# A gathered expert stage: side work emitted more thinly, one head routed alone, a fifth of the output sums on VectorE

## The chip, the cores and the metric

The kernel runs on one core of a Trainium2 chip. The metric is the device time of one execution in microseconds (us). A core has five instruction queues that matter here: PE (TensorE, matrix products), DVE (VectorE), ACT (ScalarE), POOL (GpSimd, which also issues the gathers) and SP (SyncE, which issues the weight loads). Each executes its instructions in the order fixed when the kernel is built. 16 DMA engines, shared by all queues, move data from memory.

## The reference, cut to what matters

Two transformer blocks run on 256 tokens of width 1024. The first ends in a PEER layer, a lookup in 16384 experts:

- For each token and each of 8 heads, a query is scored against two sets of 128 subkeys. The 16 best of each set give 256 candidate sums, of which the 16 best name 16 experts, with a softmax over their scores as gates ("routing").
- For each of the 8 x 16 = 128 experts of a token, the row `u` (1024 numbers) is multiplied with the token's vector and summed, passed through gelu and multiplied with the gate. The row `v` of that expert, times this number, is added to the token's output.

The second block starts with an mLSTM mixer. It treats a context of 256 tokens, which does not depend on the first block, and then the 256 tokens of the first block's output, which start from the context's final state. A mixture of 16 experts, a retention mixer and a second mixture of experts follow.

## The kernel before, in words

Tokens lie in two tiles of 128, one token per partition. The PEER stage (`peer`, L1227) has three pieces of work.

- `prepare` (L1241): eight steps, one per head. A step multiplies the tokens with a 1 MB slab of query weights on PE (L1247), copies the result, multiplies it with the subkeys, and ACT copies the scores to `sc` (L1258). Each weight half is first split into two parts by ACT and by a subtraction on DVE or POOL (L599, tile `rw`). After steps 1, 3 and 7, `route` is called for tile 0 with heads 0 to 1, 2 to 3 and 4 to 7 (L1268). After the last step tile 1 is routed, four heads at a time (L1270). Routing is almost wholly DVE work: L1343 is its first instruction and the cast at L1423 its last, which writes the row numbers for the gathers.
- `picks` (L1274): for each tile, 128 picks in pairs. POOL issues an indirect DMA (L1294) that fetches 8 KB (`u` and `v`) for each of the 128 tokens, 1 MB in all, into one of six ring buffers. DVE multiplies the `u` half with the tokens and sums (L1295, recorded at L608 as a 128x1024 instruction). Once per pair, ACT applies gelu and DVE the gate. For each pick, ACT then scales an identity matrix by the 128 weights and PE multiplies it with the `v` half, in two halves of 512 columns, summed over the 128 picks in two PSUM banks (L1305). After a tile's last pick the sum is added to `self.x[i]` (L1308).
- `context_task` (L1517): the mixer's context part. It loads the context (`load_context`, L1458), normalises it, multiplies it with 17 slabs of 1 MB (query, key, value, gates, output), and does the attention-like part for eight heads.

These three are written down in one order by `drive` (L795): every pick is worth 2600 units, and for each unit times `PACE` the side work (`prepare`, then `context_task`) is advanced by as many units as its steps claim (5200 for a slab, for example). With `PACE` 0.45 that is 1170 units per pick. Where a pick needs a head that is not routed yet, `prepare` is advanced until it is. `weave` interleaves two pieces of work in the same way.

The order written down is not the final one. When the program is built, a scheduler orders each engine's instructions: it keeps every dependency through data and through reused memory, and among what it takes to be ready it goes by the order written down. Work written late can therefore stand early on its engine, once the memory that it uses is free. Memory is handed out in the order written: `load_context` comes after the routing of tile 1 there, and its buffers reuse that routing's (offsets 8192 and up of `fa`).

The program lists each engine's work by helper lines: L592 is any ACT operation, L599 a tensor_tensor, L608 a scalar_tensor_tensor, L611 a matmul and L621 a transpose.

Of the kernel before, what the change touches and what calls it, by code (L numbers as in the profile page):

```python
# [15 lines left out]
OP = mybir.AluOpType  # L16
# [5 lines left out]

RING, BATCH = 6, 2

PACE = 0.45

RESERVE = (600, 1800)

# [465 lines left out]
class K:  # L494
# [732 lines left out]
    def peer(self):  # L1227
        h2, g = self.f(2048, True), self.bcast_row("ffn")
        self.ada_steps(99)
        self.mc = self.f(128, True)  # L1230
        h2T = self.norm_T([x.a for x in self.x], self.col("g_ffn"), sums=self.sq.a[:, :8], rows=(g, h2))
        self.sq.free(), g.free()
        self.mod_cols(0, [(n, b) for n in range(2) for b in range(2)])
        self.mod_cols(1, [(0, 0), (1, 0)])
        self.routes = [{"heads": 0, "rows": self.f(128), "gate": self.f(128), "act": self.f(128)} for _ in range(2)]
        prep = self.prepare(h2T)
        main = self.picks(h2, prep)
        self.drive(main, [self.chain(prep, self.context_task())], PACE)
        self.stream.grow(1)

    def prepare(self, h2T):  # L1241

        self.sc = [self.plain(self.RA) for _ in range(2)]
        sub = self.stream.get(("w1", 50))
        for s in range(8):
            w = self.wslab(("w1", 42 + s))
            p = self.slab_T(h2T, w)  # L1247
            q = self.f(512)
            self.act(q.a, p.a)
            p.free()  # L1250
            self.wfree(w)
            p = self.ps()
            for i in range(2):
                for f in range(2):
                    self.mm(p.a[:, i * 256 + f * 128:i * 256 + f * 128 + 128], q.a[:, f * 256 + i * 128:f * 256 + i * 128 + 128],
                            sub.a[:, (2 * s + f) * 128:(2 * s + f + 1) * 128])
            for i in range(2):
                self.act(self.sc[i].a[:, s * 256:(s + 1) * 256], p.a[:, i * 256:(i + 1) * 256])  # L1258
            p.free(), q.free()
            yield 5200  # L1260
            if s == 7:
                for b in h2T:
                    b.free()
                sub.free()
                self.stream.shrink(2)
                self.units.lo = deque([None])
            if s in (1, 3, 7):
                yield from self.route(0, {1: 0, 3: 2, 7: 4}[s], s + 1)  # L1268
        for h in (0, 4):
            yield from self.route(1, h, h + 4)  # L1270
        for b in self.sc:
            self.stream.give_back(b)

    def picks(self, h2, prep):  # L1274


        ident = self.c("ident")
        ring = dg = None
        for i, r in enumerate(self.routes):
            while r["heads"] < 1:  # L1280
                yield next(prep) * 0
            if ring is None:
                ring, dg = deque(self.f(2048, True) for _ in range(RING)), deque(self.f(128, True) for _ in range(2 * BATCH))
            po = self.ps(2)
            rows, gate, act = (r[n].a for n in ("rows", "gate", "act"))
            for k in range(0, 128, BATCH):
                while r["heads"] * 16 < k + 1:
                    yield next(prep) * 0
                got = []
                for j in range(k, k + BATCH):  # L1290
                    b = ring[0].a
                    ring.rotate(-1)
                    got.append(b)
                    self.nc.gpsimd.indirect_dma_start(b, None, self.t["puv"], bass.IndirectOffsetOnAxis(ap=rows.bitcast(U32)[:, j:j + 1], axis=0))  # L1294
                    self.stt(b[:, :1024], b[:, :1024], 1.0, h2.a[:, i * 1024:(i + 1) * 1024], OP.mult, OP.mult, accum_out=act[:, j:j + 1])  # L1295
                    yield 2600
                o = act[:, k:k + BATCH]
                self.act(o, o, AF.Gelu)
                self.tt(o, o, gate[:, k:k + BATCH], OP.mult)
                for j, b in enumerate(got):  # L1300
                    d = dg[0].a
                    dg.rotate(-1)
                    self.act(d, ident, AF.Copy, scale=act[:, k + j:k + j + 1])
                    for f in range(2):
                        self.mm(po.a[:, f * 512:(f + 1) * 512], d, b[:, 1024 + f * 512:1024 + (f + 1) * 512], k + j == 0, k + j == 127)  # L1305
            for f in range(2):
                o = self.x[i].a[:, f * 512:(f + 1) * 512]
                self.tt(o, po.a[:, f * 512:(f + 1) * 512], o, OP.add)  # L1308
            po.free()
            for n in ("rows", "gate", "act"):  # L1310
                r[n].free()
        h2.free()
        for b in (*ring, *dg):
            b.free()
# [1085 lines left out]
```

## Time and profile before

| | |
|---|---|
| time, median of 3 runs | 2660.72 us (2659.89 to 2661.95) |
| the profiled execution's own time | 2664.42 us |
| span of the profiled execution | 2662.7 us |
| PE busy / DVE busy / ACT busy / POOL busy | 87% / 46% / 28% / 24% |
| mean granted PE clock | 0.958 |
| bytes moved by DMA | 853.28 MB, mean 320 GB/s |
| of these by the POOL queue (the gathers, mostly) | 281.90 MB |

The shares are means over stages with different limits. The gathers lie between 421 and 1232 us of the span. Before them stands the first block (projections and weight products), after them the mixer's second part, the first mixture of experts, the retention mixer and the second mixture of experts. A row of the profile's windows gives, for a stretch of time, how long each engine was busy and with how many instructions, the granted PE clock (1.00 is 2.4 GHz, 0.50 is 1.2 GHz), the share of time in which the 16 DMA engines were busy, and the rate at which they moved bytes.

### The profile page before, as it was taken

How to read it: one execution, taken by the hardware profiler on the slowest of the kernel's cores; microseconds unless marked ns; L12 is line 12 of the kernel's file. 1: busy time of each engine (PE TensorE's matmuls, PEld its weight loads, DVE VectorE, ACT ScalarE, POOL GpSimd, SP SyncE). 2: the span in 40 equal slices, each digit the busy share in tenths (PEclk: the TensorE clock that was granted, in tenths of full speed). 3: DMA queues.
4: the chain of work that ended last, by engine and by line, in shares of the span. 5: the costliest groups of instructions: out<-in, count | busy, mean ns of one | idle time of the engine just before them, and what ended most of it. 6: DMA issues, size and time to landing. Idle time of an engine off the chain costs nothing. (4 is left out here: it accounts for less than half of the span.)

```text
span 2662.7 us, 32333 instructions
## 1 busy us (share of the span) xinstructions
PE 2304.7 (87%) x12327; PEld 1394.2 (52%) x12327; DVE 1236.1 (46%) x2823; ACT 751.5 (28%) x1492; POOL 626.5 (24%) x517
## 2 busy tenths in 40 slices
PE   8999987779978897777888999999879979878876
PEld 7888976325624573225876344443469963222213
DVE  4465358897855775556774112112286441000101
ACT  6554443224612642113543000000233520000000
POOL 4233433344344424433420000000033310000000
PEclk9999998889989999999998999999999989999999
DMA  7676557899999899995447999999966389999998
GB/s 281 215 250 227 208 189 279 327 349 351 352 381 396 311 351 378 416 419 208 152 146 280 390 391 409 409 409 409 361 223 211 120 317 384 409 409 409 409 409 276
DMA packets 195323, 853.28 MB, mean 320 GB/s; under 512 B 14558, under 2 KB 39726, under 8 KB 148832
## 3 DMA queue, kind: packets, MB, share of 16 engines
q1 hardware_dynamic: 153376, 569.31, 56.2%
q0 software_dynamic: 41792, 281.90, 27.7%
q8 instruction: 97, 1.59, 0.2%
q14 instruction: 58, 0.48, 0.0%
HBM read 849.97 MB, written 1.18 MB: 320 GB/s over the span
## 5 line engine op out<-in xcount | busy, mean ns | idle before, releaser
L611 PE MATMUL pp<-fa 128*128 128x512 f32 (+8 forms) x4900 | 1295.2, 497 | 221.4 <-ACT fa L592 156.7
L611 PEld LDWEIGHTS pp<-fa 128*128 128x128 f32 (+2 forms) x4900 | 561.1, 161 | 840.2 <-issue 439.4
L608 DVE SCALAR_TENSOR_TENSOR fa<-fa 128x1024 f32<-128x1024 f32 (+5 forms) x560 | 406.2, 748 | 170.9 <-DMA fa<-in_puv,fa 165.4
L611 PE MATMUL pp<-rw,rt 128*128 128x256 f32 x2928 | 401.2, 294 | 19.0 <-DVE fa L608 7.7
L611 PEld LDWEIGHTS pp<-rw,rt 128*128 128x128 f32 x2928 | 371.2, 196 | 44.3 <-issue 13.7
L1294 POOL DMA_INDIRECT fa<-in_puv,fa x256 | 278.6, 1088 | 432.3 <-PE pp L611 316.5
L599 DVE TENSOR_TENSOR fa<-pp,fa 128x512 f32<-128x512 f32 (+3 forms) x217 | 121.2, 565 | 510.7 <-PE pp L611 491.9
L592 ACT ACTIVATE fa<-fa 128x2 f32<-128x2 f32 (+9 forms) x476 | 188.0, 421 | 568.5 <-DVE fa L608 423.0
L611 PE MATMUL pp<-rt,rw 128*128 128x256 f32 x2448 | 329.4, 294 | 19.8 <-ACT rw L592 5.9
L611 PEld LDWEIGHTS pp<-rt,rw 128*128 128x128 f32 x2448 | 311.4, 198 | 35.8 <-issue 8.9
L592 ACT ACTIVATE fa<-pp 128x512 f32<-128x512 f32 (+4 forms) x164 | 93.9, 578 | 763.4 <-PE pp L611 600.7
L599 POOL TENSOR_TENSOR rw<-fa,rw 128x1024 fp32r<-128x1024 f32 x81 | 207.4, 2562 | 354.9 <-ACT rw L592 315.3
L592 ACT ACTIVATE rw<-fa 128x1024 fp32r<-128x1024 f32 x208 | 216.1, 1052 | 214.8 <-PE pp L611 124.3
L599 DVE TENSOR_TENSOR rw<-fa,rw 128x1024 fp32r<-128x1024 f32 x127 | 176.6, 1392 | 180.2 <-ACT rw L592 177.0
L611 PE MATMUL pp<-rt,fa 128*64 128x512 f32 (+3 forms) x736 | 239.7, 574 | 16.1 <-DMA rt<-in_moe_up 9.1
L611 PE MATMUL pp<-rw,fa 128*64 128x512 f32 (+2 forms) x720 | 206.4, 582 | 15.6 <-DMA rw<-in_moe_down 7.0
L605 DVE TENSOR_SCALAR fa<-pp,fa 128x128 f32<-128x128 f32 (+1 forms) x80 | 36.4, 462 | 256.9 <-PE pp L611 180.0
L599 DVE TENSOR_TENSOR fa<-fa 128x2 f32<-128x2 f32 (+13 forms) x311 | 100.3, 334 | 66.3 <-ACT fa L592 39.6
L611 PEld LDWEIGHTS pp<-rt,fa 128*64 128x64 f32 (+1 forms) x736 | 65.2, 124 | 116.9 <-issue 78.3
L611 PEld LDWEIGHTS pp<-rw,fa 128*64 128x64 f32 (+1 forms) x720 | 58.5, 123 | 126.0 <-issue 84.6
L621 PE MATMUL pp<-ct,fa 128*128 128x128 f32 (+3 forms) x425 | 72.6, 301 | 53.2 <-ACT fa L592 22.4
L1204 POOL DMA_DIRECT2D fa<-in_ada_b x4 | 2.3, 578 | 456.0 <-PE pp L611 456.0
(136 smaller groups left out, 1016.6 us busy)
## 6 DMA issues: line engine op xcount, KB each, us to landing
fa<-in_w SPq DMA_DIRECT2D x105, 1024.0 KB, 5.2
fa<-in_moe_gate SPq DMA_DIRECT2D x72, 1024.0 KB, 16.5
fa<-in_moe_down SPq DMA_DIRECT2D x68, 1024.0 KB, 16.1
fa<-in_moe_up SPq DMA_DIRECT2D x60, 1024.0 KB, 18.1
fa<-in_ada_w SPq DMA_DIRECT2D x48, 1024.0 KB, 5.4
rw<-in_moe_up SPq DMA_DIRECT2D x36, 1024.0 KB, 17.8
rt<-in_moe_down SPq DMA_DIRECT2D x31, 1024.0 KB, 14.9
rt<-in_moe_up SPq DMA_DIRECT2D x28, 1024.0 KB, 17.3
```

The lines of the kernel that those rows point to most:

```text
L592: return self.nc.scalar.activation(out, in_, func, **kw)
L599: (eng or self.nc.vector).tensor_tensor(out, a, b, op=op)
L605: (eng or self.nc.vector).tensor_scalar(out, a, s1, s2, op0=op0, op1=op1, **kw)
L608: self.nc.vector.scalar_tensor_tensor(out, a, s, b, op0=op0, op1=op1, **kw)
L611: self.nc.tensor.matmul(ps, l, r, start=start, stop=stop, skip_group_check=True)
L621: self.nc.tensor.transpose(ps, x, self.c("ident")[:k, :k])
L1204: self.nc.gpsimd.dma_start(b.a, self.t["ada_b"][1, :, s * 256:(s + 1) * 256])
L1294: self.nc.gpsimd.indirect_dma_start(b, None, self.t["puv"], bass.IndirectOffsetOnAxis(ap=rows.bitcast(U32)[:, j:j + 1], axis=0))
```

## The change

- `PACE` goes from 0.45 to 0.21, so a pick advances the side work by 546 units. The units of `prepare` are multiplied by 0.3, so its steps come at 1820 units per pick.
- The routing of tile 1 leaves `prepare` for a generator of its own, `prepare_last`. It is woven into `context_task`, 1.5 of its units for each of the context's. The context's work, its loads and its memory are therefore written down ahead of tile 1's routing and between its steps.
- `route` is called after steps 0, 1, 3 and 7 for heads 0, 1, 2 to 3 and 4 to 7 of tile 0.
- For every fifth pick (`SHARE` 5: picks 4, 9, ..., 124 of each tile, 25 per tile), one DVE instruction multiplies the `v` half with the weight and adds it to `self.x[i]`. The scaled identity on ACT and the matrix products on PE of that pick fall away.

```diff
-PACE = 0.45
+PACE = 0.21
+
+SHARE = 5
...
-        prep = self.prepare(h2T)
-        main = self.picks(h2, prep)
-        self.drive(main, [self.chain(prep, self.context_task())], PACE)
+        side = self.chain((0.3 * c for c in self.prepare(h2T)), self.weave(self.context_task(), [self.prepare_last()], 1.5))
+        self.drive(self.picks(h2, side), [side], PACE)
         self.stream.grow(1)
...
-            if s in (1, 3, 7):
-                yield from self.route(0, {1: 0, 3: 2, 7: 4}[s], s + 1)
+            if s in (0, 1, 3, 7):
+                yield from self.route(0, {0: 0, 1: 1, 3: 2, 7: 4}[s], s + 1)
+
+    def prepare_last(self):
+
         for h in (0, 4):
             yield from self.route(1, h, h + 4)
         for b in self.sc:
             self.stream.give_back(b)
...
                 for j, b in enumerate(got):
+                    if (k + j) % SHARE == SHARE - 1:
+                        self.stt(self.x[i].a, b[:, 1024:], act[:, k + j:k + j + 1], self.x[i].a, OP.mult, OP.add)
+                        continue
                     d = dg[0].a
                     dg.rotate(-1)
                     self.act(d, ident, AF.Copy, scale=act[:, k + j:k + j + 1])
```

## Rows read from the trace of the kernel before

**Rows 1.** All instructions by windows, 421 to 1200 us (busy us and count per engine).

```profile
core 0: us, PE busy (x) PEld busy (x) DVE busy (x) ACT busy (x) POOL busy (x), PEclk, DMA share, GB/s
421.00:500.00 79.00, 62.66 (x264) 41.56 (x264) 61.77 (x243) 27.87 (x58) 29.99 (x27) 0.87 0.88 337
500.00:600.00 100.00, 72.46 (x132) 28.69 (x133) 96.79 (x364) 20.79 (x57) 38.95 (x34) 0.85 0.90 339
600.00:750.00 150.00, 137.06 (x629) 89.51 (x627) 114.36 (x229) 75.20 (x139) 67.17 (x60) 0.94 0.94 350
750.00:850.00 100.00, 74.45 (x186) 32.20 (x187) 50.97 (x97) 17.96 (x58) 37.12 (x37) 0.97 1.00 408
850.00:1000.00 150.00, 138.68 (x674) 93.72 (x673) 114.50 (x282) 78.06 (x185) 58.32 (x57) 0.95 0.90 330
1000.00:1100.00 100.00, 75.89 (x176) 31.34 (x175) 52.04 (x109) 19.20 (x62) 44.12 (x38) 0.95 0.98 389
1100.00:1200.00 100.00, 74.05 (x162) 28.78 (x161) 52.59 (x100) 17.92 (x60) 38.02 (x41) 1.00 1.01 420
```

**Rows 2.** Gathers alone (L1294) by windows (busy us and count).

```profile
421.00:600.00 179.00, 62.46 (x56) 0.86 0.89 338
...
600.00:750.00 150.00, 50.11 (x42) 0.94 0.94 350
...
850.00:1000.00 150.00, 41.53 (x38) 0.95 0.90 330
...
1100.00:1200.00 100.00, 38.02 (x41) 1.00 1.01 420
```

**Rows 3.** Gathers (L1294), durations and extent; then who waited for whom, 421 to 1240.

```profile
L1294 POOL DMA_INDIRECT fa<-in_puv,fa x256: 935/939/3062, 421.5 to 1217.3; - x128
...
POOL fa L1294 <- PE pp L611: 316.5, 162, 10.6
DVE fa L608 <- DMA fa<-in_puv,fa: 165.4, 136, 6.2
```

**Rows 4.** Timelines of ACT, DVE, POOL and PE (start, us): routing and context start.

```profile
394.16 0.66 ACT L592 ACTIVATE rt<-pp 128x256 f32<-128x256 f32 x2 [0.49 <-PE pp L611]
398.34 0.49 DVE L1343 MAX8 fa<-rt 128x8 f32<-128x128 f32 x2 [1.40 <-PE pp L611]
399.08 0.64 ACT L592 ACTIVATE rt<-pp 128x256 f32<-128x256 f32 x2
421.07 0.18 DVE L1423 CAST fa<-fa 128x32 uint32<-128x32 f32 x1
520.38 0.19 DVE L1423 CAST fa<-fa 128x64 uint32<-128x64 f32 x1
595.20 0.20 DVE L1423 CAST fa<-fa 128x64 uint32<-128x64 f32 x1
596.45 0.59 POOL L1461 DMA_DIRECT2D fa<-in_ctx  x1
619.05 1.91 PE L621 MATMUL pp<-ct,fa 128*128 128x128 f32 x16
```

**Rows 5.** Instruction groups by form, 421 to 1240 us (count, busy us, mean ns).

```profile
L611 PE MATMUL pp<-fa 128*128 128x512 f32 x1024 | 503.5, 639 | 139.6 <-ACT fa L592 139.6
L608 DVE SCALAR_TENSOR_TENSOR fa<-fa 128x1024 f32<-128x1024 f32 x256 | 313.7, 1228 | 165.6 <-DMA fa<-in_puv,fa 165.4
L592 ACT ACT_TABLE_LOAD x40 | 51.3, 1283 | 5.0 <-DVE fa L608 4.1 <-DMA fa<-arow 0.2
L608 DVE DVE_READ_ACCUMULATOR fa<-fa 128x1 f32 x256 | 21.1, 82 | 0.0
```

**Rows 6.** PE's timeline: pairs of picks (8 matmuls each) after idle stretches.

```profile
521.45 6.18 PE L611 MATMUL pp<-fa 128*128 128x512 f32 x8 [4.33 <-ACT fa L592]
770.77 3.70 PE L611 MATMUL pp<-fa 128*128 128x512 f32 x8 [3.03 <-ACT fa L592]
1092.65 3.70 PE L611 MATMUL pp<-fa 128*128 128x512 f32 x8 [1.27 <-ACT fa L592]
```

## The prediction

> **What bounds the kernel now.** I read the page's slices first. The POOL queue's DMA share and the rate show a long stretch in which the gathers run. Then I read the windows over that stretch. In the last window, 1100 to 1200 us, the DMA engines are busy all the time and move 420 GB/s [rows 1], and 41 gathers are issued [rows 2], 2.44 us each. This is the floor. There the two longest waits of the stage are the ones that a full DMA leaves: POOL waits for a ring buffer that PE frees, DVE for a gather to land [rows 3]. Earlier windows fall below 420 GB/s although gathers are always open. The bytes that were not moved, as time at 420 GB/s (length x (1 - rate/420)):
>
> - 421 to 500: 79 x (1 - 337/420) = 15.6 us
> - 500 to 600: 19.3 us, with DVE busy 97%
> - 600 to 750: 25.0 us, with PE busy 91%
> - 750 to 850: 2.9 us
> - 850 to 1000: 32.1 us, with PE busy 92%
> - 1000 to 1100: 7.4 us
>
> The sum is 102.3 us [rows 1]. What fills these windows is the side work: routing on DVE until 595.2, the context's part on PE only after that. Its load is issued at 596.4, at the end of the routing of tile 1, whose memory it reuses, and its first PE work is at 619.05 [rows 4]. The stage's end sets the start of the mixer's second part, which needs all of `x`. What follows it doesn't touch the change, so I take every microsecond of this stage as one of the whole.
>
> **The change part by part.** The sum is made against the profiled execution: 2664.42 us, of which 2662.7 is the span and 1.7 lies around it. The median of the runs shown is 3.7 us below it.
>
> *One head routed alone.* The scores of step 0 leave ACT at 394.8, those of step 1 at 399.7 (start of the pair plus 0.64 to 0.66). Routing two heads runs from 398.34 to 421.25 on DVE, 22.9 us, with three weight residues (L599) between [rows 4]. One head has half the lists and half the elements. I take 13 us for it, a little over half, because the residues stay. Starting at about 395.5 it ends at 408.5, so the first gather comes 13 us earlier. Bounds: 17 us if the residues fall behind the routing, and nothing if the steps behind it are held back by as much. The second head's own routing then costs DVE again some 13 us, before pick 16.
>
> *Context ahead of tile 1's routing.* Today the two follow each other: routing of tile 1 from 520.38 to 595.20 on DVE, then the context's weight products on PE [rows 4]. In the change the context's memory is handed out first, so PE can start it at the end of the routing of tile 0, some 75 us earlier, beside tile 1's routing. The unmoved bytes of 500 to 600 (19.3 us) then overlap those of 600 to 750 (25.0 us). They would vanish if DVE had room for both. It has 36 us free in 600 to 750 [rows 1]. The two routings of tile 1 need about what is left of DVE's 96.8 us in 500 to 600 beside the picks (56 in 421 to 600 [rows 2], so some 31 here), for four fifths of that time: (96.8 - 31 x 1.31) x 0.8 = 45 us, with 1.31 for the 1.228 us of a dot and its read of the sum, 0.082 [rows 5]. So not all of it fits. I take 12 of 19.3; bounds 0 and 19.3.
>
> *Thinner emission.* Units worked out from the steps in the code: 129,900 for `prepare` after the first routing and 92,400 for the context, so today the side is written down until pick 190 (222,300/1170). In the change it is 24,500 (0.3 x 81,750 after head 0) plus 92,400, at 546 per pick, until pick 214; tile 1's routing is through at pick 115, before pick 128 needs it. That is thinner by 1.1 times in length, and by more in the context. But emission ranks work and does not place it: tile 1's routing, written from pick 62 to 111, was finished at 595, when not quite 56 gathers had been issued [rows 2]. So most of the side work will again stand as early as its memory allows. I take 8 us of the remaining 102 - 12 - 20 = 70; bounds 0 and 70. The moved steps bring their 17 loads of 1 MB on SP and their POOL work (context load, broadcasts, masks) with them. These stay inside the gather stage, in the same POOL queue between gathers, and cost what they do today.
>
> *Every fifth output on DVE.* It removes 50 x 4 matmuls and 50 identity scalings. At the full clock 8 matmuls of a pair take 3.70 us [rows 6], so a pick is 1.85. In 600 to 750 and 850 to 1000 PE is over 90% busy and 80 gathers are issued [rows 2]: 16 of them leave PE, 30 us. I take 20 us, because DVE is 76% busy there too; bounds 0 and 30. It adds 50 DVE instructions of 128x1024 with two inputs. The trace has none that adds into `x`; the nearest row is the dot of the same kind and size, 1.228 us, so 61 us in all; bounds 45 and 75. In the free stretches a pair asks DVE for 2 x 1.31 + 1.23 = 3.9 of its 4.88 us, so this is hidden. In 500 to 600 DVE has 3 us free, and 11 of the first 56 picks bring 14 us plus the split routing's fixed part, less the routing that moves to later windows. I put 7 us; bounds 0 and 30. The new instruction stands behind the gate product on DVE. Behind it waits the next dot, and for that PE, a pair later; six ring buffers cover 1.2 us.
>
> *Tables.* ACT loads a table 40 times (1.28 us each) where gelu and the context's exponentials alternate [rows 5]. Thinner mixing can add some, each of them in a pair's chain. At 257 us busy of 779, I put nothing; bound 20 us.
>
> Sum: -13 - 12 - 8 - 20 + 7 = -46 us. 2664.4 - 46 = 2618.4, and less the 3.7 us between that execution and the median: 2615 us. A measurement of this kernel tells a change apart from about 0.2%, 5 us.
>
> **The rivals.**
>
> *The filler really thins out* (chance 0.20). Then the side work fills only what PE and DVE have free beside gathers at the floor, and three quarters of the 102 us come back besides the 13: 90 us, 2571. For it: PE's whole work in 421 to 1200 is 635 us [rows 1], 85 of it goes, and DVE's 543 grows by some 70; both are below the time that the bytes need. Against it: the early place of tile 1's routing today.
>
> *The order hardly changes* (0.22). The side work stands as dense as before, the gathers stay behind it, and DVE takes as much as PE gives: only the earlier start and little more remain, 5 to 20 us, 2650. For it: the engines' orders follow memory and readiness more than emission. Against it: the memory that held the context back is no longer taken by tile 1's routing.
>
> *PE's clock falls* (0.13), the slower side. PE idles 1.27 us before a full pair in the free stretch, and 8 matmuls take 3.70 us. After 3.03 us of idling they took 3.70 as well, after 4.33 us they took 6.18, and the window 500 to 600, whose pairs stand far apart, has a granted clock of 0.85 [rows 1, 6]. A pair with one pick on DVE leaves 1.27 + 1.85 = 3.1 us idle, and two of five pairs are such. At the low level 8 matmuls take between the 6.18 seen and twice 3.70, say 6.8 us; ten picks with 8 on PE take 27.2 us instead of the 24.4 of the gathers, so the 150 or so free picks cost 42 us and the 20 us of relief do not come: -13 - 12 - 8 + 7 + 42 = +16, 2677. It decides once more than 26/0.28 = 93 picks run at the low level. Against it: 3.03 us did not lower it, and a PE that becomes the bound has no idle time.
> The Trainium skill (TensorE: Matmul & The Clock Gate, "HAM oscillation — how this bites in real kernels") warns of just this: where the compute between two DMA waits is shorter than the wait, the array goes back to the low clock at each. The trace agrees for 521 and not for 770 [rows 6]; by the rule the time would be the 2677 above.
>
> **How the numbers follow.** Forecast 0.45 (its own range 2600 to 2635), thinning 0.20, little change of order 0.22, the clock 0.13. The range from 2572 to 2668 takes in the third case, half of the second and a part of the last, and leaves out about 0.18. Faster by over 0.2% (below 2655): 0.45 + 0.20 + 0.13 of the third case = 0.78. Same: 0.08. Slower: the clock and a rest, 0.14.
>
> **What would show it.** The first gather near 408 instead of 421.5. The load of the context near 520 instead of 596, and its first PE work well before 619. In windows of the gather stage a rate above 360 GB/s wherever side work stands, and the last gather near 1172. 824 instead of 1024 matmuls of 512 columns in the stage [rows 5], and 50 more 128x1024 instructions on DVE of about 1.23 us. The forecast is wrong if the stretch from the first gather to the last stays near 796 us, if DVE is above 95% busy beyond 600, or if the granted clock in a free stretch falls below 0.9. After the last gather nothing should move but by the shift.

## The result, and the profile after

The change makes the kernel slower: 2697.35 us median (2690.44 to 2707.69), against 2660.82 before. The ratio is 1.0139 with an interval of [1.0121, 1.0158]. The profiled execution took 2700.99 us, its span is 2699.2. The forecast was 2615.

The page of the kernel after, parts 1 and 2: busy time per engine, and the span in 40 slices of 67.5 us.

```profile
PE 2282.6 (85%) x12127; PEld 1377.5 (51%) x12127; DVE 1293.6 (48%) x2899; ACT 744.0 (28%) x1447; POOL 659.5 (24%) x517
...
PEclk9999997888779997788899999999979989999998
DMA  7676548877899988998348799999966389999998
GB/s 282 210 254 234 200 181 324 331 296 284 310 366 416 343 337 329 379 380 319 115 134 306 302 397 409 409 409 409 387 239 237 103 343 356 409 409 409 409 409 268
```

The gather stage is slices 7 to 19. The granted clock stands at 7 or 8 tenths in ten of these thirteen slices, the late ones included, in which little side work stands.

The gathers of the kernel after: their durations (shortest, median, longest, ns), first and last start.

```profile
L1298 POOL DMA_INDIRECT fa<-in_puv,fa x256: 932/968/3829, 412.8 to 1261.3; - x128
```

The first gather comes 8.7 us earlier than in [rows 3], the last one 44.0 us later. The stage between them takes 848.5 us instead of 795.8. From the last gather to the end of the span it is 1437.9 us, before 1445.4. So the loss arises in the gather stage.

All instructions of the kernel after by windows, with the columns of [rows 1].

```profile
421.00:500.00 79.00, 60.01 (x259) 37.70 (x257) 66.86 (x216) 26.20 (x56) 30.01 (x22) 0.83 0.84 320
500.00:600.00 100.00, 77.94 (x271) 44.37 (x272) 90.65 (x307) 35.27 (x73) 45.61 (x37) 0.81 0.85 328
600.00:750.00 150.00, 112.38 (x463) 69.81 (x462) 127.46 (x324) 65.31 (x110) 58.36 (x50) 0.85 0.82 297
750.00:850.00 100.00, 66.92 (x117) 25.74 (x118) 57.29 (x101) 14.77 (x49) 42.84 (x37) 0.83 0.97 384
850.00:1000.00 150.00, 130.20 (x606) 87.90 (x606) 123.71 (x296) 69.72 (x168) 61.29 (x59) 0.92 0.93 351
1000.00:1100.00 100.00, 68.38 (x160) 28.74 (x158) 53.05 (x105) 22.09 (x58) 43.07 (x35) 0.83 0.90 348
1100.00:1200.00 100.00, 65.29 (x111) 25.44 (x112) 56.85 (x98) 13.71 (x47) 43.90 (x35) 0.79 0.95 378
1200.00:1240.00 40.00, 29.29 (x52) 11.16 (x51) 22.04 (x39) 6.25 (x21) 16.47 (x16) 0.81 0.95 369
```

Read the clock, then the rate. Between 1100 and 1200 PE, DVE and ACT are all far from full. Yet the rate is 378 GB/s where it was 420, at a clock of 0.79 where it was 1.00. The time of the bytes not moved at 420 GB/s, worked out as in the prediction, for before, after and four of the kernels below:

| window | before | after | sums alone | without the sums | thin alone | sums and zero column |
|---|---|---|---|---|---|---|
| 421–500 | 15.6 | 18.8 | 15.2 | 18.1 | 14.5 | 18.8 |
| 500–600 | 19.3 | 21.9 | 23.8 | 20.7 | 21.7 | 19.5 |
| 600–750 | 25.0 | 43.9 | 27.5 | 30.0 | 29.3 | 36.8 |
| 750–850 | 2.9 | 8.6 | 9.3 | 3.1 | 2.4 | 2.9 |
| 850–1000 | 32.1 | 24.6 | 31.4 | 33.2 | 24.6 | 22.1 |
| 1000–1100 | 7.4 | 17.1 | 8.8 | 6.4 | 3.1 | 2.6 |
| 1100–1200 | 0 | 10.0 | 12.4 | 0 | 1.0 | 2.6 |
| sum | 102.3 | 144.9 | 128.4 | 111.5 | 96.6 | 105.3 |

After the change 18.9 us more are lost in 600 to 750, and 25.4 us in the three windows that were nearly free (750 to 850, 1000 to 1200).

PE's timeline of the kernel after, two places in late windows (start, busy us, idle before in brackets). A pick on PE is 4 matmuls, 1.85 us at the full clock.

```profile
839.87 1.98 PE L613 MATMUL pp<-fa 128*128 128x512 f32 x4 [1.26 <-ACT fa L594]
844.82 3.70 PE L613 MATMUL pp<-fa 128*128 128x512 f32 x8 [2.96 <-ACT fa L594]
849.79 1.98 PE L613 MATMUL pp<-fa 128*128 128x512 f32 x4 [1.27 <-ACT fa L594]
854.76 3.70 PE L613 MATMUL pp<-fa 128*128 128x512 f32 x8 [2.99 <-ACT fa L594]
...
1125.22 11.31 PE L613 MATMUL pp<-fa 128*128 128x512 f32 x20 [4.15 <-ACT fa L594]
1142.99 11.14 PE L613 MATMUL pp<-fa 128*128 128x512 f32 x20 [6.45 <-ACT fa L594]
1157.37 3.68 PE L613 MATMUL pp<-fa 128*128 128x512 f32 x4 [3.25 <-ACT fa L594]
```

POOL's timeline over the second place.

```profile
1129.28 1.14 POOL L1298 DMA_INDIRECT fa<-in_puv,fa  x1 [6.68 <-PE pp L613]
1130.72 1.73 POOL L1298 DMA_INDIRECT fa<-in_puv,fa  x1 [0.30 <-issue]
...
1137.44 0.93 POOL L1298 DMA_INDIRECT fa<-in_puv,fa  x1 [0.30 <-issue]
```

At 840 to 860 the pattern is as hoped: a pair every 4.96 us, the full clock after gaps of 1.3 and 3.0 us. At 1157 one pick alone takes 3.68 us, twice its 1.85: the low level. Around it the pairs no longer come one by one. Twenty matmuls stand in one block of 11 us. DVE's timeline shows what held PE before the first of these blocks (dots are 128x1024, gate products 128x2; the rows that read a dot's sum are left out).

```profile
1114.96 0.16 DVE L601 TENSOR_TENSOR fa<-fa 128x2 f32<-128x2 f32 x1 [0.27 <-ACT fa L594]
1118.07 1.22 DVE L610 SCALAR_TENSOR_TENSOR fa<-fa 128x1024 f32<-128x1024 f32 x1 [2.94 <-DMA fa<-in_puv,fa]
1120.57 1.22 DVE L610 SCALAR_TENSOR_TENSOR fa<-fa 128x1024 f32<-128x1024 f32 x1 [1.27 <-DMA fa<-in_puv,fa]
1123.01 1.23 DVE L610 SCALAR_TENSOR_TENSOR fa<-fa 128x1024 f32<-128x1024 f32 x1 [1.22 <-DMA fa<-in_puv,fa]
1124.52 0.16 DVE L601 TENSOR_TENSOR fa<-fa 128x2 f32<-128x2 f32 x1 [0.27 <-ACT fa L594]
```

Three dots stand before this gate, where a pair needs two, and each waits for its own gather. Here the gate is *late*. PE gets nothing and idles 4.15 us; POOL waits 6.68 us for a ring buffer that PE still reads, then issues six gathers within 8.2 us. The next gate, at 1142.28, is late in the same way, and PE has idled 6.45 us by then. The block behind it takes 11.14 us for 20 matmuls (at the full clock 5 x 1.85 = 9.25): it starts low again. Each engine keeps its order, so a late gate is a matter of the order that the scheduler wrote, not of the clock. Both are therefore candidates for the loss, and the experiments have to tell them apart. Gates that are late (more dots than two per gate have run before them), of all gates in a window, counted from DVE's timelines:

| window | before | after | sums alone | without the sums | sums and zero column |
|---|---|---|---|---|---|
| 750–850 | 0 of 19 | 1 of 19 | 4 of 19 | 0 of 20 | 0 of 20 |
| 1000–1100 | 0 of 18 | 2 of 15 | 3 of 16 | 0 of 19 | 0 of 20 |
| 1100–1200 | 0 of 20 | 4 of 18 | 4 of 18 | 0 of 20 | 0 of 19 |

### The profile page after: what moved, and what is told of

Read it like the earlier page. It is cut to its first block, busy times and chain, and to the rows that moved or that the text cites. A ratio compares the mean times of both kernels' runs of the same rounds, so it can differ in the third digit from the quotient of the medians.

```text
span 2699.2 us, 31860 instructions
## 1 busy us (share of the span) xinstructions
PE 2282.6 (85%) x12127; PEld 1377.5 (51%) x12127; DVE 1293.6 (48%) x2899; ACT 744.0 (28%) x1447; POOL 659.5 (24%) x517
## 4 chain that ended last, share of the span: by engine, by line
PE 45%; DMA 22%; DVE 14%; issue 10%; ACT 4%; POOL 4%; SPq 1%; POOLq 0%; DVEq 0%; ACTq 0%
PE pp L613 44%; DMA fa<-in_puv,fa 7%; DVE fa L610 6%; DMA fa<-in_moe_down 3%; POOL fa L1298 3%; ACT fa L594 2%; DMA rw<-in_moe_down 2%; DVE fa L601 2%; DVE rw L601 1%; DMA rt<-in_moe_up 1%; DMA rw<-in_moe_up 1%; DMA rw<-in_moe_gate 1%; DMA fa<-in_moe_up 1%; DMA fa<-in_moe_gate 1%; PE pp L623 1%
## 5 line engine op out<-in xcount | busy, mean ns | idle before, releaser
L613 PE MATMUL pp<-fa 128*128 128x512 f32 (+8 forms) x4700 | 1270.7, 507 | 268.7 <-ACT fa L594 200.5
L613 PEld LDWEIGHTS pp<-fa 128*128 128x128 f32 (+2 forms) x4700 | 548.9, 165 | 878.1 <-issue 431.4
L610 DVE SCALAR_TENSOR_TENSOR fa<-fa 128x1024 f32<-128x1024 f32 (+6 forms) x611 | 472.5, 798 | 180.3 <-DMA fa<-in_puv,fa 172.6
L613 PE MATMUL pp<-rw,rt 128*128 128x256 f32 x2928 | 395.6, 292 | 29.5 <-ACT rw L594 10.6
L1298 POOL DMA_INDIRECT fa<-in_puv,fa x256 | 312.7, 1221 | 439.6 <-PE pp L613 306.4
L601 DVE TENSOR_TENSOR fa<-fa 128x2 f32<-128x2 f32 (+12 forms) x325 | 99.0, 317 | 70.2 <-ACT fa L594 44.7
```

The source lines that it names most:

```text
L601: (eng or self.nc.vector).tensor_tensor(out, a, b, op=op)
L610: self.nc.vector.scalar_tensor_tensor(out, a, s, b, op0=op0, op1=op1, **kw)
L613: self.nc.tensor.matmul(ps, l, r, start=start, stop=stop, skip_group_check=True)
```

## The experiments

**The sums alone.** Theory: the DVE sums are the loss. Rival: the new order is.

```diff
 # before.py
+SHARE = 5
+                    if (k + j) % SHARE == SHARE - 1:
+                        self.stt(self.x[i].a, b[:, 1024:], act[:, k + j:k + j + 1], self.x[i].a, OP.mult, OP.add)
+                        continue
```

> The kernel before with every fifth output on VectorE and nothing else of the change. Theory 1 (the lighter TensorE falls to its low clock between pairs of picks): the granted clock in the free stretches before and after the mixer's work falls to about 0.8 as in the changed kernel, the rate there from 420 to about 365 GB/s, and the time is 2675 to 2695 us. Theory 2 (the loss is the crowding of the context's work with tile 1's routing on VectorE, and the sums on VectorE are hidden): 2640 to 2662 us, with a clock of at least 0.95 in the free stretches.

Measured: 2702.46 us, 1.0151 [1.0104, 1.0198]; stage 826.0 us. Its windows:

```profile
750.00:850.00 100.00, 64.24 (x114) 25.07 (x115) 56.93 (x100) 14.71 (x49) 41.76 (x35) 0.84 0.96 381
...
1100.00:1200.00 100.00, 66.74 (x116) 25.96 (x116) 55.02 (x96) 14.10 (x47) 46.75 (x38) 0.81 0.94 368
```

In the old order the sums alone give the whole loss, with the same low clock in free stretches. The time lies 7 us above the range expected for the clock. Late gates are there too, so this run doesn't tell clock and order apart.

**The change without the sums.** The four new lines of the first diff are taken out of the kernel after.

> The changed kernel with all outputs back on TensorE: the thin emission and the head routed alone stay. Theory 1 (clock): 2655 to 2670 us, free stretches at 420 GB/s and clock 0.95 or more. Theory 2 (crowding): 2685 to 2700 us, since the order in which context and routing stand is kept. If both hold, about 2675 us.

Measured: 2655.84 us, 0.9978 [0.9957, 0.9998]; stage 810.0 us.

```profile
600.00:750.00 150.00, 123.92 (x502) 74.88 (x500) 127.08 (x329) 67.66 (x125) 61.92 (x55) 0.94 0.89 336
...
1100.00:1200.00 100.00, 74.47 (x163) 28.96 (x162) 52.61 (x102) 18.01 (x60) 37.57 (x40) 1.00 1.01 421
```

The new order of the side work is harmless, and the last window is at the floor again. Against this kernel the sums cost 1.61%, some 43 us of 2661.

**PE kept busy, the sums left on DVE.** This is to separate the clock from DVE's load. For each shared pick PE also multiplies its rows by zeros, which adds nothing to the result. In the first version the zeros were a matrix of their own; in the second they are one constant column, broadcast, which takes no memory.

```diff
 # after.py, in the branch of SHARE
                         self.stt(self.x[i].a, b[:, 1024:], act[:, k + j:k + j + 1], self.x[i].a, OP.mult, OP.add)
+                        for f in range(2):
+                            self.mm(po.a[:, f * 512:(f + 1) * 512], self.c("tlt")[:, :1].to_broadcast([128, 128]), b[:, 1024 + f * 512:1024 + (f + 1) * 512], False, False)
                         continue
```

> The changed kernel, and for every fifth pick TensorE also multiplies the fetched rows with a matrix of zeros into the same sum, so that its number of matrix products is that of the kernel before while the sums on VectorE stay. Theory 1 (clock): the free stretches go back to a clock of 0.95 or more and 410 to 420 GB/s, and the time is 20 to 30 us below the changed kernel, 2667 to 2677 us, though TensorE does more. Theory 2 (crowding), under which TensorE's work only delays: 2697 to 2710 us.

> As the run with products by a matrix of zeros, but the zeros are a constant column read 128 times, so that no memory is taken and the later stages are laid out as in the changed kernel. In that earlier run the gather stage went from 848 to 813 us and the stages after it became 18 us longer. Theory 1 (clock): gather stage 810 to 820 us again, the rest as in the changed kernel (1438 us after the last gather), together 2660 to 2670 us. Theory 2 (the instructions on VectorE themselves cost what is left): 2680 to 2690 us.

Measured: with the matrix 2685.17 us, 1.0084 [1.0061, 1.0108]; stage 813.2. With the column 2667.8 us, 1.0025 [1.0005, 1.0046]; stage 802.2. The stages after the last gather differ by 13 us between the two (1456.4 and 1443.0), so the second is the one to read. Its windows:

```profile
600.00:750.00 150.00, 125.76 (x572) 81.80 (x570) 138.72 (x354) 75.96 (x126) 59.01 (x50) 0.92 0.87 317
...
1000.00:1100.00 100.00, 75.80 (x165) 30.51 (x164) 61.95 (x121) 20.16 (x58) 44.44 (x41) 0.95 1.00 409
1100.00:1200.00 100.00, 76.89 (x160) 30.63 (x158) 61.56 (x106) 14.70 (x49) 41.52 (x40) 0.95 1.00 409
```

PE's timeline of the same kernel (the matmuls that read `ct` are the zero products):

```profile
1118.25 1.88 PE L613 MATMUL pp<-fa,ct 128*128 128x512 f32 x4
1120.00 1.99 PE L613 MATMUL pp<-fa 128*128 128x512 f32 x4
1124.96 3.70 PE L613 MATMUL pp<-fa 128*128 128x512 f32 x8 [2.98 <-ACT fa L594]
1129.93 1.98 PE L613 MATMUL pp<-fa 128*128 128x512 f32 x4 [1.27 <-ACT fa L594]
1131.75 1.88 PE L613 MATMUL pp<-fa,ct 128*128 128x512 f32 x4
```

With the zero column the time is 30 us lower (1.0139 to 1.0025), though PE does more; the version with the matrix stays between the two expected ranges. The clock is 0.95 to 0.97 in the free stretches, the pairs come mostly one by one there, and the rate is 408 to 409. But the edit changes two things: PE is fed, and no gate of the free stretches is late any more (table above). The zero products read the shared pick's buffer; whether that is why the scheduler writes another order was not tried. Where no side work stands and the order is the same, the two kernels can be compared: from 755 to 835 DVE has only dots, gates and sums in both traces, none late. First the kernel after, then the zero column.

```profile
755.00:835.00 80.00, 56.34 (x97) 21.51 (x95) 44.80 (x79) 11.55 (x39) 34.93 (x30) 0.81 0.95 375
...
755.00:835.00 80.00, 59.64 (x125) 23.71 (x124) 49.01 (x85) 12.30 (x41) 36.22 (x31) 0.96 1.01 416
```

In the same order, the kernel at 0.81 moves 375 GB/s and the one at 0.96 moves 416. The kernel after has 373 GB/s at 0.81 from 1200 to 1260, where again no gate is late, and no more than that, 373 at 0.79, from 1060 to 1200 with six late ones. So at the low clock the whole loss of rate is there without late gates. Some 300 us of free stretches (755 to 835 and 1040 to 1261) at 375 instead of 416 make 29 us, an estimate; the three windows of the table differ by 27.6 (35.7 to 8.1). What the late gates add, or whether they set off the low stretch after 1040, stays open.

What stays of the loss against the kernel without sums is 0.47%, 12 us. I take it for the sums' own time, which no run shows by itself: DVE is busy 92% of 600 to 750, where the rate is 317 against 336. The profiled execution of the zero column took 2659.72 us, 8 below its median, that of the kernel without the sums 2664.84, 9 above; their stage lengths should not be set against each other.

**The same in the old order.** Sums and zero column in the kernel before.

> Every fifth output on VectorE in the kernel before's order (no thin emission, two heads first), with products by a constant column of zeros that keep TensorE's count. Theory 1 (clock): most of the 40 us that the share alone cost is back, 2662 to 2675 us, gather stage 795 to 805 us instead of 826. Theory 2: 2690 to 2702 us.

Measured: 2690.48 us, 1.0107 [1.0078, 1.0136]; stage 810.4.

```profile
500.00:600.00 100.00, 67.42 (x127) 27.03 (x127) 99.76 (x392) 20.77 (x50) 39.05 (x31) 0.86 0.86 324
...
1100.00:1200.00 100.00, 76.67 (x157) 30.60 (x155) 60.63 (x104) 14.70 (x49) 44.02 (x39) 0.93 1.00 409
```

Only 12 us of 40 come back; the time lies in the range expected if the clock were not the cause. The stage is 15.6 us shorter than with the sums alone. But of the free stretches only the last is at 409; 750 to 850 stays at 388 with a clock of 0.88. DVE is full from 500 to 600, and the stages behind the last gather take 12 us more than before (1457.7 from the last gather to the end; with the sums alone 1452.7, before 1445.4). Why those later stages, which the edit does not touch, differ by such amounts is open.

**Even halves.** In four of five pairs the second pick's second 512 columns go to DVE instead of whole fifth picks; so PE has 6 matmuls in such a pair and never only 4.

```diff
 # after.py, SHARE taken out
-                    for f in range(2):
+                    n = 1 if j and k % 10 != 6 else 2
+                    if n == 1:
+                        self.stt(self.x[i].a[:, 512:], b[:, 1536:], act[:, k + j:k + j + 1], self.x[i].a[:, 512:], OP.mult, OP.add)
+                    for f in range(n):
```

> The changed kernel, but the same fifth of the products leaves TensorE evenly: in four of five pairs, the second half (512 columns) of the second pick is added on VectorE, and no pick leaves TensorE whole. TensorE then idles 2.2 us before a pair in a free stretch instead of 1.3 or 3.0. Theory 1 (clock, through the uneven gaps): clock at least 0.95 and 415 to 420 GB/s in the free stretches, gather stage 790 to 810 us, 2640 to 2660 us. Theory 2 (any work moved to VectorE costs): 2680 to 2700 us. If the mean load of TensorE counts and not the single gap, the clock stays near 0.8 and the time near 2695 us.

Measured: 2681.78 us, 1.0073 [1.0045, 1.0102]; stage 827.2. PE's timeline:

```profile
1106.39 2.84 PE L613 MATMUL pp<-fa 128*128 128x512 f32 x6 [2.13 <-ACT fa L594]
1111.36 4.54 PE L613 MATMUL pp<-fa 128*128 128x512 f32 x6 [2.13 <-ACT fa L594]
```

The same DVE elements, spread evenly, cost about half. The clock did not stay at 0.95 as the theory of the uneven gaps wanted: it is 0.83 to 0.88 in the free stretches, with 404, 365 and 403 GB/s in the three windows (before 408, 389 and 420). None of their gates is late, so this too is loss at a low clock without late gates. Two neighbouring pairs after the same gap of 2.13 us ran at different clocks. So no length of a single gap in these traces divides the two levels.

**One pick of every pair.** SHARE at 2: 63 picks of each tile on DVE.

> The changed kernel with every second pick on VectorE (63 per tile) instead of every fifth: each pair leaves one pick on TensorE, so its gaps are about 3.1 us in every pair of a free stretch. Theory 1 (the cost comes from full pairs at the low clock, 6 to 7 us against the 4.9 us in which two gathers land): the granted clock there is lower than in the changed kernel, 0.5 to 0.7, and yet the gathers run at 410 to 420 GB/s, because one pick takes under 4 us even at the low clock. If the low clock costs by itself, the rate there is below 380 GB/s. In the crowded windows VectorE is overloaded by some 126 sums of 1.23 us, so the whole time is open, 2660 to 2710 us.

Measured: 2680.43 us, 1.0074 [1.0053, 1.0094]; stage 823.1. Its windows, then PE's timeline:

```profile
600.00:750.00 150.00, 103.77 (x521) 74.08 (x519) 139.99 (x353) 59.51 (x92) 62.07 (x44) 0.78 0.82 302
...
1100.00:1200.00 100.00, 57.83 (x81) 18.13 (x81) 76.06 (x121) 12.10 (x40) 61.48 (x40) 0.77 1.01 421
```

```profile
1108.69 3.57 PE L613 MATMUL pp<-fa 128*128 128x512 f32 x4 [3.00 <-ACT fa L594]
1113.67 1.98 PE L613 MATMUL pp<-fa 128*128 128x512 f32 x4 [1.41 <-ACT fa L594]
```

This run corrects the simple story. The clock of this window is the lowest of all kernels, 0.77 (0.5 to 0.7 was expected), and the rate is at its floor, 421 GB/s. A low clock costs nothing where a pair's work on PE, 3.57 us for one pick, still fits in the 4.9 us in which two gathers land. A full pair, 8 matmuls, does not: at the low level it would take some twice 3.57, 7.1 us. The loss here is in 600 to 750 instead, with DVE at 93%, and goes on to 780, where side work ends.

**The parts without sums.** Thin emission alone (context ahead, `weave`, PACE 0.21; heads 0 and 1 together, no sums), and the single head alone:

```diff
 # before.py, head alone
-            if s in (1, 3, 7):
-                yield from self.route(0, {1: 0, 3: 2, 7: 4}[s], s + 1)
+            if s in (0, 1, 3, 7):
+                yield from self.route(0, {0: 0, 1: 1, 3: 2, 7: 4}[s], s + 1)
```

> The kernel before with the thin emission alone (PACE 0.21, the routing of tile 1 woven into the context); two heads are routed first and all outputs are on TensorE. Theory 1 (clock): 2650 to 2665 us. Theory 2 (crowding): 2690 to 2705 us. Against the run without the share it tells what the head routed alone is worth: about 9 us less there by the earlier first gather of the changed kernel (412.8 instead of 421.5), if that is kept to the end.

> The kernel before with the first head of tile 0 routed alone, nothing else of the change. The first gather comes 7 to 9 us earlier. If that is kept: 2652 to 2656 us. From the runs without the share (with and without the head alone) I expect that it is lost again, because the second routing takes VectorE time before pick 16: 2660 to 2668 us.

Measured: thin alone 2652.83 us, 0.9961 [0.9939, 0.9983], stage 790.0; head alone 2659.25 us, 1.0001 [0.9983, 1.0018], stage 799.9, first gather at 413.9. Thin alone has the lowest median of all and beats both kernels; its interval overlaps that of the kernel without the sums. Its windows:

```profile
500.00:600.00 100.00, 85.19 (x348) 51.54 (x349) 87.78 (x268) 35.60 (x79) 41.84 (x37) 0.94 0.84 329
600.00:750.00 150.00, 123.94 (x510) 75.65 (x509) 121.08 (x326) 75.91 (x133) 62.27 (x59) 0.92 0.89 338
...
850.00:1000.00 150.00, 136.50 (x623) 88.69 (x624) 112.97 (x279) 75.06 (x176) 56.37 (x55) 0.95 0.92 351
1000.00:1100.00 100.00, 75.19 (x169) 29.14 (x167) 54.22 (x115) 23.14 (x71) 41.19 (x41) 0.98 0.99 407
```

DVE falls from 97% to 88% in 500 to 600, but the rate falls too (329, before 339). What thinning gains it gains later: 351 against 330 and 407 against 389 between 850 and 1100.

**Two variants of the thin kernel.** One adds a zero product of 512 columns after each of the first 32 pairs, to raise the clock before 600. The other sets PACE from 0.21 to 0.30, which emits the side work denser.

> The thin emission alone (the fastest so far, ratio 0.996 to the kernel before), and after each of the first 32 pairs of tile 0 one product of 512 columns by a constant column of zeros, to keep TensorE's clock up where it is 0.87 (421 to 500 us). Theory 1 (clock): clock at least 0.93 from 421 to 600, up to 8 us saved there, 2643 to 2652 us. If VectorE is what holds these windows, no change or up to 5 us more: 2652 to 2660 us.

> The thin emission alone with PACE 0.30 instead of 0.21. If the emission only sets the ranks among ready work and the gain comes from the context's memory standing ahead of tile 1's routing, the time is that of PACE 0.21 within 5 us, 2648 to 2660 us. If the thinness itself gives the gain, it shrinks by about half: 2655 to 2662 us.

Measured: 2670.18 us, 1.0036 [1.001, 1.0063], stage 807.9; and 2666.75 us, 1.0015 [1.0001, 1.0029], stage 787.2. The first raised the clock of 500 to 600 from 0.94 to 0.97 and the rate from 329 to 340, and lost it in 600 to 750 (318 against 338). Zero products that helped a starved PE did not help here. Both times lie above every range expected. The second has the shorter stage and is still 14 us slower than thin alone: it loses 16 us behind the last gather (1457.7 against 1441.7). In the gather stage the denser emission is as good as the thinner, so the thin kernel's 0.4% is not shown to come from thinness.

## Why the prediction was wrong, point by point

The step that failed is **every fifth output on DVE**: it was put at -20 us, with the crowding on DVE at +7 beside it, and the two together measured +43 (1.0139 against 0.9978). For the free stretches it said "so this is hidden" and put the cost at nothing; there alone 25.4 us more were lost. Three things bear on it.

- *What PE loses with the work.* The prediction counted 30 us of relief where PE is over 90% busy. The runs showed that PE's load is also what keeps its clock up. Taken off, the clock falls to 0.79 to 0.83 in the free stretches, full pairs become longer than the gathers' step, buffers come free late, and the floor of 420 GB/s is lost: 375 at 0.81 against 416 at 0.96 in the same order. This was the slower rival, with a chance of 0.13 and a price of 42 us for the clock. Its mechanism held, its price was somewhat high: some 30 us by the zero column, and an upper bound, as that edit also took the late gates away.
- *What was said against that rival.* "3.03 us did not lower it" held in the undisturbed rhythm (2.99 us at 854, full clock). It did not hold where the rhythm was disturbed. Gaps of 4.15 and 6.45 us then stand behind late gates, an order that the prediction did not foresee: it looked at what waits behind the new instruction, not at what the scheduler writes around it. "A PE that becomes the bound has no idle time" fell too: POOL waits for buffers that PE holds, while PE waits for a gate. As I read these waits, the bound is then neither engine but the loop of PE, POOL and the gathers through the six ring buffers.
- *DVE's crowding* was +7; the 12 us that stay with the zero column are its nearest measure, and the window that shows it most is 600 to 750. The price of an instruction was right: estimated 1.23 us, and the trace has

```profile
1127.19 2.42 DVE L610 SCALAR_TENSOR_TENSOR fa<-fa 128x1024 f32<-128x1024 f32 x2
```

a sum and the dot behind it in 2.42 us. The stage has 804 recorded matmuls of 512 columns for the 824 worked out (a few per cent of them can be missing from a trace) and 301 instructions of 128x1024 for 306.

The Trainium skill (TensorE: Matmul & The Clock Gate, "HAM oscillation — how this bites in real kernels") describes a loop whose compute is shorter than its wait for data, so that each step starts at the low clock. The trace agrees in part: the blocks behind the waits of 4.15 and 6.45 us start low, though PE's work before them was longer (5.40 and 11.31 us). It does not tell these cases apart: the same 2.13 us once with and once without the full clock, and the 421 GB/s at a clock of 0.77.

The other steps:

- *One head alone* (-13): the first gather did come 8.7 us earlier, 413.9 in the kernel with nothing else changed. But the stage behind it was 4 us longer and the time is the same, 1.0001. The bound of nothing was the answer, and the reason named with it fits: tile 1's routing, among the steps behind, ended at 604.6 instead of 595.2.
- *Context ahead of tile 1's routing* (-12) and *thinner emission* (-8): together -10 us (0.9961). The move took place as forecast: the context's loads are issued at 516.58 and 527.60 (before at 586.01 and 596.45; the prediction had only the second), its first PE work is at 538.97 instead of 619.05. But the 19.3 us of 500 to 600 did not vanish; the table has 21.7 there for thin alone. The 11.8 us that do come back lie between 850 and 1100 (39.5 to 27.7). DVE had been freed to 88%, so its fullness was not what had limited that window, or not alone.
- *Tables* (0): 45 loads instead of the 40 of [rows 5], 6.4 us on an engine that is a third busy. Right.
- *After the last gather nothing moves*: from the last gather to the end it takes from 7.5 us less than before (the kernel after) to 12.3 us more (sums and zero column in the old order), which no step had foreseen. The cause is open.

## What to carry to other kernels

Before taking work off TensorE in a loop paced by DMA, work out its step at the low clock. If a step at the low clock is still shorter than the transfers it waits for, moving work is safe; if only the step at the full clock fits, the relief can cost more than the load did. A few products by zero in the freed place test whether the clock is the cause, if the order of the other engines is compared as well: here it changed with them. And test the parts of a bundled change apart: here one part of three was worth 0.4%, and another hid it.

## What the runs showed of the hardware that was not expected

- With useless work on PE the kernel was faster: 50 groups of 4 zero matmuls, 1.88 us each, and 30 us less, though a part may be the order on DVE that came with them.
- The granted clock alone is a poor witness: 0.79 went with 378 GB/s, 0.77 with 421. Only beside the work of a step does it say anything.
- The disturbed rhythm can keep itself going: from 1200 to 1260 the kernel after stays at 0.81 and 373 GB/s with no late gate. It can also end: from 840 to 860 the clock is 1.00 and the rate 422.
- 128 more floats of memory per partition (the zero matrix) went with stages after the gathers that took 13 us longer than with the column. Whether by memory, by order or by the spread of single executions was not tried.
